# Two squared-relu sections merged, small loads a stage ahead, and contractions padded to 128 rows

## The chip, the cores and the metric

The kernel runs on one core of one Trainium2 chip. The metric is the device time of one launch in microseconds, 2791.74 before the change. Five engines work side by side, each through its own instructions in order: TensorE (PE: matrix products and transposes), VectorE (DVE), ScalarE (ACT), GpSimd (POOL) and SyncE (SP), which here only issues transfers between the chip's main memory and the on-chip memory (SBUF). TensorE writes its results to banks of a small accumulator memory (PSUM), and VectorE or ScalarE takes them from there.

## What is computed

A sequence of 512 tokens of width 1024 goes through two blocks, all in float32. The first block has two layers, latent attention with a squared-relu part and then a gated recurrence with another. The second block adds three mixers (sparse attention with a top-k index, "dsa"; compressed, selected and windowed attention, "nsa"; a state-space scan, "ssd") and ends with a squared-relu part of its own.

```python
def sq_relu_mlp(h, w1, w2):            # 1024 -> 4096 -> 1024
    a = jax.nn.relu(h @ w1)
    return (a * a) @ w2

for layer in range(DEPTH):             # DEPTH = 2: mla_mixer, then hgrn2_mixer
    ...
    h = h + rms_norm(m, norm_gains[layer, 1])
    a = rms_norm(h, norm_gains[layer, 2])
    h = h + rms_norm(sq_relu_mlp(a, mlp_w1[layer], mlp_w2[layer]), norm_gains[layer, 3])

# second block
u = rms_norm_2(x, norm1_g) @ w_in      # split into the inputs of the mixers
# dsa: idx = relu(iq . ik) weighted by iw (8 heads of 32), top-k keys, softmax over them
# nsa: blocks = a[:, win_idx] + pos; compress = einsum('bnlgd,lde->bnge', blocks, w)
# ssd: dt = softplus(dt + dt_bias); a = -exp(a_log); a_cum = cumsum(dt * a)
#      y_diag from exp(a_cum_i - a_cum_j), then the scan over 4 chunks of 128 tokens
```

## The kernel before

**Stages.** `build` (L2040) runs five stages one after another: the latent attention, the first squared-relu part (`mlp0`, about 232 to 584 us in the trace), the recurrence (`hgrn`, to 892 us), the second squared-relu part (`mlp1`, to 1253 us) and the second block (`b2`). The tokens are in NT = 4 blocks of 128. The input of a stage lies transposed in SBUF as `xT`, in a high and a low part.

**Products.** A float32 product is three matmuls of rounded parts: high by high, high by low, low by high (`mm3`, L124 to L126). Weights arrive as `raw` tiles over the one queue of SP and are split by `chunk`: ScalarE casts the high part (L209), VectorE or GpSimd subtracts the low part (L210; GpSimd while the last token blocks of a stage are still to be moved). `raw` tiles come from a ring of two (`wr`), chunks from a ring of four (`wc`), or, for the first ones of a stage, from a pool of large tiles (`b8`).

**A squared-relu stage** (`mlp`, L511) runs eight sections. Section s computes 512 of the 4096 hidden columns with `dense_a` (weights moving, the transposed input fixed), evacuates them by relu, square and split into `hT` (L524 to L527), and multiplies them by 512 rows of `w2` with `run_section`. The result has two halves of 512 columns per token block, each a sum over 4 k-tiles of 128, added to the accumulator `acc` by VectorE (L440; the first section copies by ScalarE, L438).

**The bridge** (`bridge`, L428) joins a stage to the next. After each half of a token block in the last section it squares and sums (`half`, L462), takes the reciprocal root on ScalarE and VectorE (L160 to L163), multiplies by a gain (L478, GpSimd for the first two token blocks), updates the residual h (L487) and writes the next stage's normalized input (L494). One token block later `move` (L502) transposes it on TensorE (L399) and splits it again (L129, L130). The moves of the last two blocks are left to the next stage's first products.

**The second block** begins with `dense_b` for the columns that dsa needs (`first[tb]`). `ssd_consts` (L1602) is called there: it loads the small operands of the scan (`conv_w`, `conv_b`, `norm_g` through a transpose, L176 to L180; `dsk` by two loads L1613, 64 partitions by 16 single elements each; `dtb` and `na` as rows repeated over 128 partitions, L1116) and `time_steps` (L1633) computes dt and its sums on VectorE, ScalarE and TensorE. `dsa` (L1262) and `nsa` (L1369) load small gains of their own (`gk`, `gqd`, `pos`). In dsa the index queries and keys are packed as high, low, high in `ipk` (three parts of 32 columns: 96 rows after the transposes L1294 and L1300) for the index products L1314. In nsa a compressed value `vc4` of 32 rows stands four times, and L1586 multiplies 32 of its 128 rows; the compressed keys and values come from `mm3` over split sums `bs` (L1480, L1481). TensorE has matmuls of later weights ("fill") between these steps.

What sets the order: a scheduler places the instructions on each engine when the kernel is built, so the tables of the section on the change show the built order.

## Time and profile before

| | us |
|---|---|
| runs shown | 2789.57, 2791.74, 2791.75; median 2791.74 |
| profiled execution | 2790.97, its span 2789.3, granted TensorE clock 0.983 of full |
| busy in the span | TensorE 2656.4 (95%), VectorE 1641.2 (59%), ScalarE 1211.7 (43%), GpSimd 496.4 (18%) |
| chain of work that ended last | TensorE 80%, VectorE 11%, ScalarE 4%, issue 2%, transfers 1%, GpSimd 1% |

The chain is followed back from the last instruction, each step to what released it. TensorE is on it four fifths of the time; what the other engines hold of it are the places where TensorE stands idle and waits for them, and these are found in the list of waits and in the timelines of single engines. The granted clock of a stretch tells whether TensorE's matmuls ran at its upper level there.

### The profile page before, as it was taken

To read this page: it belongs to the slowest core of one execution; us is meant where nothing else is said; L and a number is where in the kernel's file an instruction comes from. 1 tells how busy PE (TensorE), PEld (TensorE's weight loads), DVE (VectorE), ACT (ScalarE), POOL (GpSimd) and SP (SyncE) were. 2 spreads that over 40 slices of the span, in tenths; PEclk is the share of its full clock that TensorE was granted. 3 is DMA by queue.
4 is the path that set the end of the run, shared out by engine and by line. 5 is a ranking of instruction groups with operands and counts; after the bars stand their busy time and mean duration, and the time that the engine had idled before them with its cause. 6 is when DMAs were issued, how large, how long until landed. Compare 5 with 4: busy or idle time off the path is not lost.

```text
span 2789.3 us, 35203 instructions
## 1 busy us (share of the span) xinstructions
PE 2656.4 (95%) x13393; PEld 2190.2 (79%) x13393; DVE 1641.2 (59%) x3231; ACT 1211.7 (43%) x2389; POOL 496.4 (18%) x370
## 2 busy tenths in 40 slices
PE   7999999989999999996899989989999999999999
PEld 6888888868888888875677777777788887888887
DVE  6755444466565444453976659759748774544444
ACT  5555222245454322232457536636645652232222
POOL 1010000020002000012322213212365556200000
PEclk9999999999999999998999999999999999999999
DMA  4232322322233223323331231211152335222332
GB/s 138 61 121 76 101 96 91 106 69 83 69 114 106 91 91 101 96 88 97 99 92 47 89 88 57 61 57 50 59 183 84 108 112 181 98 91 91 104 93 76
DMA packets 281965, 259.09 MB, mean 93 GB/s; under 512 B 39436, under 2 KB 224068, under 8 KB 281796
## 3 DMA queue, kind: packets, MB, share of 16 engines
q1 hardware_dynamic: 281796, 256.84, 29.7%
q8 instruction: 105, 1.72, 0.3%
q14 instruction: 64, 0.52, 0.1%
HBM read 234.79 MB, written 22.02 MB: 92 GB/s over the span
## 4 chain that ended last, share of the span: by engine, by line
PE 80%; DVE 11%; ACT 4%; issue 2%; DMA 1%; POOL 1%; SPq 0%; ACTq 0%; DVEq 0%; POOLq 0%
PE pm L124 20%; PE pm L125 20%; PE pm L126 20%; PE po L606 2%; PE psc L126 2%; PE psc L124 2%; PE psc L125 2%; PE pt L601 2%; PE psc L1896 1%; PE psc L1060 1%; ACT wch L209 1%; DMA gk<-in_dsa_k_norm_dram 1%; PE pt L399 1%; POOL wch L210 1%; DVE qraw L1161 1%
## 5 line engine op out<-in xcount | busy, mean ns | idle before, releaser
L209 ACT CAST wch<-raw 128x1024 fp32r<-128x1024 f32 (+3 forms) x393 | 407.6, 1041 | 497.3 <-PE pm L126 392.6
L124 PE MATMUL pm<-xT,wch 128*128 128x512 f32 (+1 forms) x1568 | 597.9, 383 | 2.2 <-ACT xT L129 1.5
L125 PE MATMUL pm<-xT,wch 128*128 128x512 f32 (+1 forms) x1568 | 596.3, 381 | 0.9 <-DVE xT L130 0.9
L126 PE MATMUL pm<-xT,wch 128*128 128x512 f32 (+1 forms) x1568 | 595.4, 380 | 1.3 <-POOL wch L210 1.3
L210 DVE TENSOR_TENSOR wch<-raw,wch 128x1024 fp32r<-128x1024 f32 (+1 forms) x266 | 325.5, 1225 | 196.7 <-ACT wch L209 196.3
L210 POOL TENSOR_TENSOR wch<-raw,wch 128x1024 fp32r<-128x1024 f32 (+3 forms) x127 | 307.9, 2429 | 702.2 <-ACT wch L209 669.7
L124 PEld LDWEIGHTS pm<-xT,wch 128*128 128x128 f32 x1568 | 296.4, 190 | 55.2 <-ACT xT L129 3.2
L126 PEld LDWEIGHTS pm<-xT,wch 128*128 128x128 f32 x1568 | 297.4, 190 | 53.4 <-POOL wch L210 1.7
L125 PEld LDWEIGHTS pm<-xT,wch 128*128 128x128 f32 x1568 | 297.7, 190 | 52.4 <-DVE xT L130 2.0
L124 PE MATMUL pm<-wch,hT 128*128 128x512 f32 x768 | 300.1, 393 | 0.2 <-ACT hT L526 0.2
L125 PE MATMUL pm<-wch,hT 128*128 128x512 f32 x768 | 295.5, 390 | 0.0
L126 PE MATMUL pm<-wch,hT 128*128 128x512 f32 x768 | 295.5, 390 | 0.0
L525 DVE SCALAR_TENSOR_TENSOR f<-pm,r 128x512 f32<-128x512 f32 x96 | 66.4, 691 | 249.8 <-ACT r L524 249.6
L524 ACT ACTIVATE r<-pm 128x512 f32<-128x512 f32 x96 | 57.4, 598 | 322.4 <-PE pm L126 322.4
L124 PEld LDWEIGHTS pm<-wch,hT 128*128 128x128 f32 x768 | 144.2, 188 | 38.0 <-ACT hT L526 8.8
L126 PEld LDWEIGHTS pm<-wch,hT 128*128 128x128 f32 x768 | 143.5, 188 | 31.0
L125 PEld LDWEIGHTS pm<-wch,hT 128*128 128x128 f32 x768 | 144.2, 188 | 29.2
L478 POOL TENSOR_TENSOR acc<-acc,g 128x512 f32<-128x512 f32 x16 | 21.3, 1335 | 695.9 <-ACT bj L462 353.4
L562 ACT ACTIVATE p<-p,mn 128x128 f32<-128x128 f32 x224 | 125.7, 566 | 20.9 <-DVE mn L560 19.8
L440 DVE TENSOR_TENSOR acc<-pm,acc 128x512 f32<-128x512 f32 x112 | 77.1, 689 | 95.5 <-PE pm L126 95.1
L130 DVE TENSOR_TENSOR pT<-pt,pT 128x512 fp32r<-128x512 f32 x224 | 100.5, 485 | 30.1 <-ACT pT L129 28.1
L129 ACT CAST pT<-pt 128x512 fp32r<-128x512 f32 x224 | 86.0, 428 | 45.1 <-PE pt L601 29.6
(570 smaller groups left out, 4857.2 us busy)
## 6 DMA issues: line engine op xcount, KB each, us to landing
raw<-in_mlp_w_dram SPq DMA_DIRECT2D x64, 1024.0 KB, 5.3
raw<-in_w_in_dram SPq DMA_DIRECT2D x64, 512.0 KB, 3.7
raw<-in_w_ff_dram SPq DMA_DIRECT2D x32, 1024.0 KB, 5.2
raw<-in_hgrn_w_in_dram SPq DMA_DIRECT2D x24, 512.0 KB, 4.2
raw<-in_w_in_dram SPq DMA_DIRECT2D x8, 1024.0 KB, 5.9
raw<-in_w_br_ssd_dram SPq DMA_DIRECT2D x16, 512.0 KB, 4.2
gd<-fo SPq DMA_DIRECT2D x24, 256.0 KB, 2.3
fg<-gd SPq DMA_DIRECT2D x24, 256.0 KB, 3.1
```

What stands on the lines that cost most here:

```text
L124: mm(p, ah, bh, start=start, stop=False)
L125: mm(p, ah, bl, start=False, stop=False)
L126: mm(p, al, bh, start=False, stop=stop)
L129: self.nc.scalar.copy(h, src)
L130: self.nc.vector.tensor_sub(l, src, h)
L209: self.nc.scalar.copy(w[:, 0], raw)
L210: (self.nc.gpsimd if self.late and LP else self.lo).tensor_sub(w[:, 1], raw, w[:, 0])
L440: self.nc.vector.tensor_add(d, p, d)
L524: nc.scalar.activation(r, p, AF.Relu)
L525: nc.vector.scalar_tensor_tensor(f, p, 0.0, r, op0=ALU.max, op1=ALU.mult)
L562: nc.scalar.activation(p, p, AF.Exp, bias=mn[:, b:b + 1], scale=-1.0, accum_out=sm[:, b:b + 1])
L601: nc.tensor.transpose(t[:, (b - kb) * 128:(b - kb + 1) * 128], p[b][:, kb * 128:kb * 128 + 128], self.ident)
```

## The change

Sections 6 and 7 of `mlp0` and `mlp1` become one: section 6 keeps its `hT`, and after section 7's `dense_a` one `run_section` sums over 8 k-tiles of 128. Its second column half takes its chunks from a pool of four (`mlpw`) in `mlp0`, and from the pool of large tiles in `mlp1`. `ssd_consts` becomes `small_operands`; it is called at the start of `mlp1`, and the gains and positions of dsa and nsa are loaded there as well. The adds of `dtb` stay at the start of the second block; the rest of `time_steps` becomes part of `late_sums`, which is called behind the top-k. `ipk` gets four parts, so the index products contract 128 rows; `vc4` holds its 32 rows in four places of a zeroed 128-row tile; `acumT` and `sel` go from 96 rows to 128. The compressed keys and values are 16 plain float32 matmuls instead of 48 of split parts.

```diff
     def chunk(self, raw, pool=None, early=False):
-        if early:
+        if early or pool is self.big:
...
-    def mlp(self, X, w1, w2, g_out, g_next, alloc=None):
+    def mlp(self, X, w1, w2, g_out, g_next, alloc=None, begin=None):
...
+            if begin:
+                begin(self.sc, tmp)
+            X2 = lambda tiles: lambda k, hl: tiles[k // 4][hl][:, k % 4]
+            held = []
...
+                held.append(hT)
+                if s == 6 and g_out is not None:
+                    continue
+                pools = None, None
                 if s == 7:
                     if g_out is not None:
                         bridge = self.bridge(st, acc, g_out, g_next, alloc)
+                        pools = None, self.big if alloc else self.pool("mlpw", 4, st)
...
-                self.run_section(w2, s * 4, lambda k, hl: hT[hl][:, k], 4,
-                             self.add_to(acc, s == 0 and g_out is not None), (lambda: bridge) if bridge else None)
+                n = len(held)
+                self.run_section(w2, (s + 1 - n) * 4, X2(held), 4 * n,
+                                 self.add_to(acc, s == 0 and g_out is not None), (lambda: bridge) if bridge else None, pools)
+                held = []
...
-                self.ssd_consts(sc, first)
+                self.time_steps(first)
...
-                    pk = ip.tile([128, 9, 3, 32], F32R, name="ipk")
+                    pk = ip.tile([128, 9, 4, 32], F32R, name="ipk")
...
+                    for a in range(2):
+                        nc.scalar.copy(pq[:, :, a, 0], src[:, 0:8])
+                    nc.vector.tensor_sub(pq[:, :, 0, 1], src[:, 0:8], pq[:, :, 0, 0])
+                    nc.vector.tensor_sub(pq[:, :, 1, 1], src[:, 0:8], pq[:, :, 0, 0])
...
-                self.late_sums()
                 self.normed_keys(ip, kraw, 1, NT, lambda i: gk, lambda i: kh[:, 0], lambda i: kl[:, 0])
...
                     nc.vector.tensor_scalar(ix, ix, -2e38, -NEG, op0=ALU.is_gt, op1=ALU.mult)
+                self.late_sums()
...
-                    w = self.chunk(self.raw(A["nsa_cmp_w_2"][0, i].rearrange("(k l) d e -> (l d) k e", l=2)))
+                    w = self.raw(A["nsa_cmp_w_2"][0, i].rearrange("(k l) d e -> (l d) k e", l=2))
...
-                    bs = ip.tile([128, 2, 16, 32], F32R, name="bs")
-                    nc.scalar.copy(bs[:, 0], bl)
-                    nc.vector.tensor_sub(bs[:, 1], bl, bs[:, 0])
                     p = self.sbank()
                     for k in range(16):
-                        self.mm3(p[:32, :64], bs[:, 0, k], bs[:, 1, k], w[:, 0, k], w[:, 1, k], k == 0, k == 15)
+                        nc.tensor.matmul(p[:32, :64], bl[:, k], w[:, k], start=k == 0, stop=k == 15)
...
+                        nc.gpsimd.memset(vc4.bitcast(F32), 0.0)
                         for a in range(4):
-                            nc.scalar.copy(vc4[32 * a:32 * a + 32], vc)
+                            nc.scalar.copy(vc4[32 * a:32 * a + 32, a], vc)
...
-                    r = slice(32 * (i % 4), 32 * (i % 4) + 32)
                     for hl in range(2):
-                        nc.tensor.matmul(po, vc4[r], pcT[i // 4][r, hl], start=hl == 0, stop=False)
+                        nc.tensor.matmul(po, vc4[:, i % 4], pcT[i // 4][:, hl], start=hl == 0, stop=False)
...
-    def ssd_consts(self, pl, first):
+    def small_operands(self, pl, tmp):
...
+        dk = self.bc_row(pl, A["dsa_k_norm_2"][0], 64, "gk")
+        dq = raw("r")
+        nc.sync.dma_start(dq[:, :64], bc_rows(A["dsa_q_norm_2"][0], 64))
+        nc.sync.dma_start(dq[:, 64:], bc_rows(A["nsa_q_norm_2"][0], 64))
...
-            at = pl.tile([96, S], F32R, name="acumT")
-            sel = pl.tile([96, 32], F32R, name="sel")
+            at = pl.tile([128, S], F32R, name="acumT")
+            sel = pl.tile([128, 32], F32R, name="sel")
...
-            rb = self.fl.tile([128, S], F32, name="rb", tag="rb", bufs=1)
+            rb = self.b8([4, S], F32, "rb")[:, 0]
...
+            k.sc = k.pool("sc", 1, right, side="right")
...
-                X = k.mlp(X, A["mlp_w1"][j], A["mlp_w2"][j], ng[j, 3], g, alloc(nxt))
+                X = k.mlp(X, A["mlp_w1"][j], A["mlp_w2"][j], ng[j, 3], g, alloc(nxt), k.small_operands if nxt == "b2" else None)
```

ScalarE at the end of the first squared-relu stage, before: squares and sums of the bridge (L462, of `acc` and of h), reciprocal roots (L160), casts of moved blocks (L129) and of the next stage's weights (L209).

```order
L462 ACTIVATE bj,bss<-acc 128x512
L209 CAST wch<-raw 128x1024
L462 ACTIVATE bj,bss<-h 128x512
L160 ACTIVATE ry<-bs_4832,eps 128x1
L462 ACTIVATE bj,bss<-h 128x512
L129 CAST xT<-pt 128x4x128
L209 CAST wch<-raw 128x1024
L160 ACTIVATE ry<-bs_4848,eps 128x1
L129 CAST xT<-pt 128x4x128
L462 ACTIVATE bj,bss<-acc 128x512
```

The same place in the changed kernel.

```order
L462 ACTIVATE bj,bss<-h 128x512
L160 ACTIVATE ry<-bs_4795,eps 128x1
L462 ACTIVATE bj,bss<-h 128x512
L209 CAST wch<-raw 128x1024
L160 ACTIVATE ry<-bs_4811,eps 128x1
L209 CAST wch<-raw 128x1024 x3
L462 ACTIVATE bj,bss<-acc 128x512
L129 CAST xT<-pt 128x4x128
L462 ACTIVATE bj,bss<-acc 128x512
L129 CAST xT<-pt 128x4x128
```

The four casts of weights stood among three steps of the chain before, and stand around one reciprocal root now; on TensorE the second of the four moves stands 15 matmuls behind the first before and 48 now.

SP at the start of the second squared-relu stage, before: the gains of the bridge, the weights of the stage, the gains of the next bridge.

```order
L452 DMA g_7129<-in_norm_gains_dram 128x1024
L455 DMA g_7131<-in_norm_gains_dram 128x1024
L200 DMA raw<-in_mlp_w_dram 128x8x256 x2
L200 DMA raw<-in_mlp_w_dram 128x4x512 x2
L452 DMA g_9623<-in_norm_gains_dram 128x1024
L455 DMA g_9625<-in_norm_g_dram 128x1024
```

The same place in the changed kernel, from the bridge's second gain on.

```order
L455 DMA g_7119<-in_norm_gains_dram 128x1024
L1612 DMA dsk<-in_ssd_d_dram 64x16x1 x2
L1128 DMA dtb<-in_ssd_dt_bias_dram 128x32
L1128 DMA na<-in_ssd_a_log_dram 128x32
L1128 DMA gk<-in_dsa_k_norm_dram 128x64
L1633 DMA gk_7484<-in_nsa_k_norm_dram 128x64 x3
L200 DMA raw<-in_mlp_w_dram 128x8x256 x2
L200 DMA raw<-in_mlp_w_dram 128x4x512 x2
L176 DMA r<-in_ssd_conv_w_dram 96x128
L176 DMA r<-in_ssd_conv_b_dram 24x128
```

The small loads stand between the bridge's gains and the stage's first weights, and behind these come the inputs of the scan's convolution.

ScalarE at the same place, before: the split of the last weights of the recurrence, its accumulator copies and squares.

```order
L209 CAST wch<-raw 128x1024 x4
L438 COPY acc<-pm 128x512
L209 CAST wch<-raw 128x1024
L462 ACTIVATE bj,bss<-acc 128x512
L438 COPY acc<-pm 128x512
L209 CAST wch<-raw 128x1024 x2
L438 COPY acc<-pm 128x512
L462 ACTIVATE bj,bss<-acc 128x512 x2
L160 ACT_TABLE_LOAD
```

The same place in the changed kernel, where L1617 is the exponential of `na`.

```order
L209 CAST wch<-raw 128x1024 x4
L1617 ACTIVATE na<-na 128x32
L438 COPY acc<-pm 128x512
L462 ACTIVATE bj,bss<-acc 128x512
L438 COPY acc<-pm 128x512
L209 CAST wch<-raw 128x1024 x2
L438 COPY acc<-pm 128x512
L462 ACTIVATE bj,bss<-acc 128x512
L209 CAST wch<-raw 128x1024
L160 ACT_TABLE_LOAD
```

The exponential stands ahead of the first copy L438, and one cast L209 comes later by two rows.

## Rows read from the trace of the kernel before

**Rows 1.** The page, part 1: busy us (share of span) and instructions.
```profile
PE 2656.4 (95%) x13393; PEld 2190.2 (79%) x13393; DVE 1641.2 (59%) x3231; ACT 1211.7 (43%) x2389; POOL 496.4 (18%) x370
```

**Rows 2.** Timeline of TensorE: start, us, what, [idle before, releaser], three places.
```profile
594.07 1.94 PE L399 MATMUL pt<-ident,acc 128*128 128x128 f32 x8 [9.95 <-DVE acc L494]
...
1261.86 1.94 PE L399 MATMUL pt<-ident,acc 128*128 128x128 f32 x8 [9.04 <-DVE acc L494]
...
1330.64 0.34 PE L1294 MATMUL pt<-identr,ipk 128*96 128x128 f32 x1 [24.62 <-DVE ipk L1291]
```

**Rows 3.** Busy time by windows: us, then each engine, PEclk, DMA share, GB/s.
```profile
584.00:598.00 14.00, 4.05 (x15) 3.48 (x15) 13.21 (x16) 5.77 (x12) 8.99 (x8) 0.64 0.36 113
1305.00:1336.00 31.00, 6.38 (x28) 5.14 (x27) 15.14 (x46) 8.95 (x25) 8.16 (x4) 0.56 0.39 122
1700.00:1790.00 90.00, 89.23 (x519) 72.72 (x518) 79.42 (x262) 68.83 (x198) 25.39 (x22) 1.00 0.10 27
```

**Rows 4.** Timeline of VectorE and of GpSimd at the end of the first squared-relu stage.
```profile
591.10 3.48 DVE L494 SCALAR_TENSOR_TENSOR acc<-h,ry,g 128x512 f32<-128x512 f32 x2
...
588.22 5.16 POOL L210 TENSOR_TENSOR wch<-raw,wch 128x1024 fp32r<-128x1024 f32 x2 [2.50 <-issue]
```

**Rows 5.** Timeline of VectorE at the start of the second block.
```profile
1318.81 0.39 DVE L1639 TENSOR_TENSOR fo<-psc,dtb 128x32 f32<-128x32 f32 x3 [21.86 <-DMA gk<-in_dsa_k_norm_dram]
```

**Rows 6.** DMA issues, 1284 to 1324 us: count, KB each, median us to landing.
```profile
dsk<-in_ssd_d_dram SPq DMA_DIRECT2D x2, 4.0 KB, 18.6
...
na<-in_ssd_a_log_dram SPq DMA_DIRECT2D x1, 16.0 KB, 19.9
```

**Rows 7.** Timeline of SyncE's DMA issues at both places.
```profile
843.56 0.34 SPq L455 DMA_DIRECT2D g<-in_norm_gains_dram  x1
...
1293.63 1.44 SPq L1613 DMA_DIRECT2D dsk<-in_ssd_d_dram  x2
...
1299.01 1.15 SPq L1116 DMA_DIRECT2D na<-in_ssd_a_log_dram  x1
```

**Rows 8.** Timeline of ScalarE at the end of the recurrent stage.
```profile
865.57 0.59 ACT L438 COPY acc<-pm 128x512 f32<-128x512 f32 x1 [5.11 <-PE pm L126]
```

**Rows 9.** TensorE's waits, 855 to 912 us: us in total, times, longest.
```profile
PE pt L399 <- DVE acc L494: 2.9, 2, 1.7
```

**Rows 10.** The page, parts 5 (busy, mean ns, idle) and 6 (us to landing).
```profile
L209 ACT CAST wch<-raw 128x1024 fp32r<-128x1024 f32 (+3 forms) x393 | 407.6, 1041 | 497.3 <-PE pm L126 392.6
...
L210 DVE TENSOR_TENSOR wch<-raw,wch 128x1024 fp32r<-128x1024 f32 (+1 forms) x266 | 325.5, 1225 | 196.7 <-ACT wch L209 196.3
...
raw<-in_mlp_w_dram SPq DMA_DIRECT2D x64, 1024.0 KB, 5.3
```

**Rows 11.** Timeline of TensorE around matmuls over 32 rows.
```profile
1687.02 0.40 PE L125 MATMUL pm<-xT,wch 128*128 128x512 f32 x1
1687.35 0.49 PE L1586 MATMUL po<-pcT,vc 32*128 32x512 f32 x1
1687.77 0.50 PE L126 MATMUL pm<-xT,wch 128*128 128x512 f32 x1
1688.10 0.40 PE L124 MATMUL pm<-xT,wch 128*128 128x512 f32 x1
1688.34 0.39 PE L125 MATMUL pm<-xT,wch 128*128 128x512 f32 x1
...
1721.45 0.73 PE L1586 MATMUL po<-pcT,vc 32*128 32x512 f32 x2
1722.11 0.92 PE L606 MATMUL po<-pT,vsw 128*128 128x512 f32 x3
```

**Rows 12.** Groups by line and form, L1586: count, ns least, median, most.
```profile
L1586 PE MATMUL po<-pcT,vc x32: 382/492/590, 1686.0 to 1986.6; 32*128 32x512 f32 x32
```

**Rows 13.** TensorE's waits over the whole span.
```profile
PE psc L124 <- ACT bs L1480: 3.5, 2, 2.1
...
PE psc L126 <- DVE bs L1481: 1.7, 1, 1.7
```

More of the change, by code (lines that the diff above doesn't have):

```diff
@@ L1623, in ssd_consts, with time_steps @@
                                 channel_multiplier=-1)
-        ones = pl.tile([128, 128], F32, name="ones2")
+        ones = pl.tile([128, 1], F32, name="ones2")
         nc.gpsimd.memset(ones, 1.0)
-        cwf = cw.rearrange("p a b -> p (a b)")
-        nc.vector.tensor_scalar(cwf, cwf, 0.5, None, op0=ALU.mult)
-        self.sc = cw, gn, dsk, tri, ones, *self.time_steps(pl, tri, ones, dtb, na, first)
-    def time_steps(self, pl, tri, ones, dtb, na, first):
+        dk = self.bc_row(pl, A["dsa_k_norm_2"][0], 64, "gk")
+        dq = raw("r")
+        nc.sync.dma_start(dq[:, :64], bc_rows(A["dsa_q_norm_2"][0], 64))
+        nc.sync.dma_start(dq[:, 64:], bc_rows(A["nsa_q_norm_2"][0], 64))
+        nc.vector.scalar_tensor_tensor(dk, dk, -0.125, dq[:, :64], op0=ALU.mult, op1=ALU.mult)
+        gk = pl.tile([128, 3, 64], F32, name="gk3")
+        for i in range(3):
+            nc.sync.dma_start(gk[:, i], bc_rows(A["nsa_k_norm_2"][0, i], 64))
+        nc.vector.tensor_mul(gk, gk, dq[:, None, 64:].to_broadcast([128, 3, 64]))
+        nc.vector.tensor_scalar(gk, gk, -0.125, None, op0=ALU.mult)
+        posr = tmp.tile([128, S], F32, name="f")[:16, :256].rearrange("p (a c) -> p a c", a=2)
+        pos = pl.tile([128, 2, 16], F32, name="pos")
+        for i in range(2):
+            nc.sync.dma_start(posr[:, i], A["nsa_cmp_pos_2"][0, i].rearrange("(k l) d -> k (l d)", l=2))
+        t = self.tbank()
+        for i in range(2):
+            nc.tensor.transpose(t[:, i * 16:i * 16 + 16], posr[:, i], self.ident[:16, :16])
+        nc.vector.tensor_copy(pos, t[:, :32].rearrange("p (i k) -> p i k", k=16))
+        steps = tuple(pl.tile([128, NT, 32], F32, name=n) for n in ("dt", "acum", "dtd", "cd"))
+        self.sops = (cw, gn, dsk, tri, ones, *steps), dtb, na, dk, gk, pos
+    def time_steps(self, first):
         nc = self.nc
-        dt, acum, dtd, cd = (pl.tile([128, NT, 32], F32, name=n) for n in ("dt", "acum", "dtd", "cd"))
+        (_, _, _, tri, ones, dt, acum, dtd, cd), dtb, na = self.sops[:3]
         q, x = (self.fl.tile([128, S], F32, name=n, tag=n) for n in ("fg", "fo"))
@@ L1676, in ssd @@
             xt8 = lambda shape, dt, name: xp.tile([128] + shape, dt, name=name, tag="b8")
-            cw, gn, dsk, tri, ones, dt, acum, dtd, cd = self.sc
+            cw, gn, dsk, tri, ones, dt, acum, dtd, cd = self.sops[0]
             def conv(m, p, c):
@@ L1697, in conv @@
                 return c
[L1700 to L1702 removed]
+            at = pl.tile([128, S], F32R, name="acumT")
+            sel = pl.tile([128, 32], F32R, name="sel")
+            for a in range(4):
                 nc.scalar.copy(sel[32 * a:32 * a + 32], self.ident[:32, :32])
@@ L1911, in ssd_pair @@
             t = self.tbank()
-            nc.tensor.matmul(t, sel[:, h:h + 1].to_broadcast([96, 128]), at, start=True, stop=True)
+            nc.tensor.matmul(t, sel[:, h:h + 1].to_broadcast([128, 128]), at, start=True, stop=True)
             L = tr("L")
```

86 lines of the change are left out of this document (35 added, 51 removed).

## The prediction

> **What bounds the kernel now.** I read the totals first [rows 1]: TensorE works 2656.4 of 2789.3 us, so a local edit can win only idle TensorE time, slow-clock time or matmul time. The profiled execution took 2790.97 us, 1.7 more than its span; the median of the runs shown is 2791.74, 0.8 more, so a sum made against the profiled one stands for both within 0.1%. Next I read the three longest idle stretches of TensorE [rows 2]: 9.95 us at the end of the first squared-relu stage, 9.04 at the end of the second, and 24.62 in the first microseconds of the second block. Together they are 43.6 of 132.9 idle us. Work at the half clock follows them [rows 3]: the mean granted clock over the first and the third stretch is 0.64 and 0.56 (its levels are 1.2 and 2.4 GHz), where in the attention of the second block 89.23 of 90 us are busy at 1.00.
>
> What ends last in each? At the ends of the stages it is VectorE's L494, the next stage's normalized input [rows 4]. Two L494 take 3.48 us, while GpSimd runs the weight-splitting subtractions of L210, two of them in 5.16. So the idle 9.95 us is a chain of short VectorE steps that GpSimd stretches, with too few products left to cover it. At the start of the second block it is a transfer: VectorE's first add on dtb waited 21.86 us [rows 5]. The two dsk loads, of 4 KB each at most, land 18.6 us after issue, and the loads queued behind them (na 19.9 us) wait too [rows 6, 7].
>
> **Part A, sections 6 and 7 in one.** It removes eight accumulator adds per stage, beside TensorE's work: worth nothing. What counts is the bridge. A token block's products were 24 matmuls by 0.23 us [rows 11] = 5.5 us; with 8 k-tiles they are 48, 11 us, so the chain for one block hides under the next block's products, and 48 instead of 15 matmuls lie between the first two moves. Yet the four casts of the next stage's weights and their L210 still stand ahead of block 1's L162, L163 and L494, so the stretched steps remain. The nearest row is the end of the recurrent stage, whose last products already have 8 k-tiles: 2.9 us in two waits [rows 9]. I take 3.4 left of each gap.
>
> Per stage, the old loss is the gap and about 2 us of work at half clock after it (4.05 us busy in the first stretch [rows 3], most of it at half speed): 12 and 11. The new section has a wait of its own. Four raw weight tiles are wanted where two were, and the ring holds two. The third is asked for when the second has been split, so the path is split 1.04 + 1.22, landing 5.3, split 2.26 [rows 10]: 9.8 us, against 36 matmuls by 0.23 = 8.2 us. That leaves 1.6, taken as 2 in the first stage. In the second stage the chunks come from the pool that still holds the input of dense_a, and two casts wait ahead of the last relu; by the same rows 1.04 us for the relu and about 3.5 for a chunk's cast, subtraction and first use, 4.6 together. Clock dips, up to 2 us for each wait that remains or is new, as after the old gaps, take 2.5 and 2. Gain 12 - 3.4 - 2 - 2.5 = 4.1 and 11 - 3.4 - 4.6 - 2 = 1: **5 us**. Bounds: 20 when only the recurrent stage's 2.9 us remains of 23; 5 lost when the chain keeps its length and the new waits come on top.
>
> **Part B, small operands a stage ahead.** Start of the second block: the 24.62 us gap loses its cause. What is next? TensorE has 21 fill matmuls, 4.8 us, before the first index transpose. In the new order VectorE's adds need no transfer and the index subtraction comes twelve rows behind them, some 3 us. I expect 0 to 2 us left, and 2 us more come back from the half clock (6.38 us busy in 31 at 0.56 [rows 3]): gain **25**, bounds 18 and 29.
>
> Start of the second squared-relu stage pays. The loads now stand on SP behind g1 and g2, the second issued at 843.56 [rows 7], and ahead of the four weight loads. dsk would be asked for at about 844.4. From dsk's issue, 1293.63, to na's landing, 1299.01 + 19.9, it took 25.3 us [rows 6, 7], some 2 of them behind two weight tiles, so na lands at 867 to 870. On ScalarE na's Exp now stands ahead of the first accumulator copy L438, which ran at 865.57 after 5.11 idle us [rows 8] and freed the bank that TensorE's next product needs. So TensorE stops for 2 to 4.5 us; the evacuations, L462 and casts queued behind the Exp come as much later, and so do the weight loads, which now wait for dsk's landing near 863 (844.4 + 18.6). With one dip and the first square and sum of the bridge coming late: **7 lost**, bounds 0 (na lands by 865.5) and 14 (the 4.5 us are paid a second and a third time at the two moves, with a dip). The transposes of conv_w and pos stand inside the stage's first dense part, whose loads land near 900 us; 0 to 3, I take **1 lost**. na's other use, the time steps, moves behind the top-k with cover by fill matmuls: nothing.
>
> **Part C, 128-row contractions.** Thirty-two matmuls L1586 contract 32 rows [rows 12]. From the matmul before an isolated one the starts are 0.33, 0.42 and 0.33 us apart, and then 0.24 between 128-row neighbours [rows 11]: 1.08 - 3 x 0.23 = 0.39 lost. A pair takes 0.66 where 0.46 would do (last two lines of [rows 11]); with 0.10 on either side as above that is 0.40. Four single and fourteen paired places make 18 by 0.40 = 7.2. TensorE has no slack there (89.23 of 90 us busy [rows 3]), VectorE has some (79.42): of 7.2 I take **6**, bounds 3 and 7.2. The 96-row contractions are left at nothing.
>
> The row speaks against overlap: two 32-row matmuls in a row take 0.66 us, not the time of one. The Trainium skill ("TensorE: Matmul & The Clock Gate", Why this matters for your kernels) advises the opposite of this change, slicing small contractions into separate 32-row groups because such matmuls then run concurrently. Here both of a pair sit in one group, so no overlap was there to lose; had it been, the pairs' overlap would be lost, 14 by 0.23 = 3.2 us slower instead of 6 faster, and the sum would be 2768. The Trainium skill ("TensorEngine Tiling (Array Packing)", Key Properties) states that changing the tiling mode drains TensorE, which this trace's 0.33 and 0.42 us at a change, against 0.24, agree with.
>
> The compressed keys lose the cast L1480 and subtraction L1481, and GpSimd's chunk subtraction; TensorE waited 3.5 and 1.7 us for these two [rows 13]. What is next is the 16 adds on VectorE ahead of them, so part stays: **4**, bounds 2 and 7 with the dips. Their matmuls fall from 48 cheap ones to 16 in plain float32, whose price here I bound at plus or minus 1. More copies for the 128-row index tiles lie beside fill matmuls: nothing.
>
> Sum: 2790.97 - 5 - 25 + 7 + 1 - 6 - 4 = **2759**; by the parts' bounds, not all at one end, 2745 to 2775.
>
> **Rivals.** First, the merge hides nearly everything and na comes in time: A 20, B 26, C 10, 2735. For it: the recurrent stage's small waits. Against it: the two-tile ring.
>
> Second, the wait for dsk moves rather than goes: SP, ScalarE and the weight tiles stall at the second squared-relu stage for 20 us instead of 8. Then 2790.97 - 5 - 25 + 20 + 1 - 10 = 2772. For it: the dsk loads are as small and as scattered there. Against it: ScalarE is free from 860 to 865 us, so most of the landing is covered.
>
> Third, the merge does not do what it says: the chain keeps both gaps whole and the new waits of 2 + 4.6 with a dip each are added: 10 lost in place of 5 gained, 2774.
>
> Fourth, slower than before: na's Exp at the head of ScalarE's order. The other terms gain 39; so it decides from a landing later than about 905 us, 39 us behind the copy at 865.57. If the DMA engines served the two first weight loads along with dsk (10.6 us) and dsk itself took twice its 18.6, na would land near 899: 33 us, with the 14 of the moves 47, and 2799. Against it: dsk is first in the queue.
>
> **How the numbers follow.** Forecast 0.54, first rival 0.16, second 0.13, third 0.12, fourth 0.03; 0.02 for anything else. The likeliest gives 2759. The range reaches down to 2742, most of the way to the first rival, and up to 2778, past the second and third. About 0.2%, 5.6 us, is what a measurement of this kernel can tell from no change: faster holds the forecast, the first and most of the two middle rivals, 0.91; same 0.05, from the middle rivals together; slower 0.04.
>
> **What would show it.** A: waits for L494 at the ends near 3 us, and a wait on a chunk in the merged section's second half. B: no idle stretch above 3 us at the index transposes, dsk's landing some 18 us after an issue near 844, and a TensorE wait near 866. C: starts 0.23 us apart around the matmuls that were L1586 (L1582 in the changed kernel). The forecast is wrong if the gaps at the stages' ends are still 9 us, if the stall near 866 exceeds 10, or if the attention of the second block does not shorten by some 3 us per group.

## The result, and the profile after

The changed kernel takes 2746.7 us, the median of four runs (2743.34 to 2748.76), against 2791.74: ratio 0.9834 [0.9816, 0.9853], 45 us faster. The forecast was 2759 in a range of 2742 to 2778: the direction was right and the range held the time, but the forecast was 12 us too slow. The profiled execution took 2748.3 us, 1.7 more than its span. Both profiled executions stand within 2 us of their medians, so differences between the two traces can be read as differences of the kernels. Executions of one kernel lie up to 16 us apart, the longer ones at a lower granted clock (a_only, below: 2771 to 2773 us at 0.987 or 0.988, 2782 to 2785 at 0.982), so a difference of medians is good to some 5 us, and the leads in the traces are read beside it.

From the page of the changed kernel, its span and its part 1, which answers to [rows 1]:

```profile
span 2746.6 us, 35061 instructions
...
PE 2652.5 (97%) x13329; PEld 2192.9 (80%) x13329; DVE 1619.0 (59%) x3211; ACT 1204.4 (44%) x2382; POOL 498.6 (18%) x373
```

TensorE's busy time fell by only 3.9 us (64 matmuls fewer) and the span by 42.7. Nearly all of the gain is idle TensorE time: 132.9 us before, 94.1 now.

The list of TensorE's waits in the changed kernel (engine, what waits, releaser: us in total, times, longest), of three windows: the ends of the first and the second squared-relu stage, and the start of the second block. They answer to the three rows of [rows 2], of 9.95, 9.04 and 24.62 us.

```profile
PE pt L399 <- DVE acc L494: 3.1, 2, 2.1
```
```profile
PE pt L399 <- DVE acc L494: 2.1, 2, 1.9
```
```profile
PE pt L1307 <- DVE ry L153: 5.3, 1, 5.3
PE pt L1307 <- DVE rt L151: 1.3, 1, 1.3
```

Each of the three shrank and none went to nothing. At the end of the recurrent stage, where [rows 9] had 2.9 us of waits, the same list (855 to 912 us) now has a new first line:

```profile
PE pm L124 <- ACT acc L438: 4.3, 1, 4.3
```

For a balance, take the moment at which the same piece of TensorE's work starts in both traces; their difference is the changed kernel's lead.

| place | before, us | after, us | lead | change of lead |
|---|---|---|---|---|
| end of the latent attention, last move | 239.9 | 239.5 | 0.4 | |
| end of first squared-relu stage, last move | 619.3 | 610.9 | 8.4 | +8.0 |
| end of recurrence, last move | 910.9 | 910.4 | 0.5 | -7.9 |
| end of second squared-relu stage, last move | 1282.5 | 1274.0 | 8.5 | +8.0 |
| second block, first index product | 1336.4 | 1298.3 | 38.1 | +29.6 |
| dsa, last product with its values | 1564.6 | 1535.1 | 29.5 | -8.6 |
| nsa, keys | 1595.9 | 1563.4 | 32.5 | +3.0 |
| nsa, first product with vc4 | 1686.0 | 1646.1 | 39.9 | +7.4 |
| nsa, last one of the first group | 1776.0 | 1731.3 | 44.7 | +4.8 |
| nsa, last one of the second group | 1986.6 | 1937.5 | 49.1 | +4.4 |
| end | 2785.2 | 2742.8 | 42.4 | -6.7 |

Part of the lead at the start of the second block is order, not gain. Busy time by windows over that stretch (us; then PE, PEld, DVE, ACT, POOL busy with counts; PE clock, DMA share, GB/s), the kernel before and then the changed one:

```profile
1282.50:1336.40 53.90, 27.34 (x120) 21.73 (x119) 17.74 (x52) 15.24 (x33) 15.69 (x7) 0.75 0.43 122
```
```profile
1274.00:1298.30 24.30, 16.20 (x74) 12.52 (x71) 19.15 (x49) 12.07 (x28) 11.96 (x5) 0.89 0.85 249
```

TensorE's idle time goes from 26.6 to 8.1 us, 18.5 less. Busy time falls by 11.1, because 46 matmuls of fill no longer stand ahead of the first index product; they are still done, later. At 0.227 us each these are 10.4 us, which leaves 0.7 for the better clock. The next stretch, to the last product of dsa, shows where they went:

```profile
1336.40:1564.60 228.20, 216.25 (x1119) 172.19 (x1117) 172.21 (x460) 137.44 (x327) 63.28 (x68) 0.99 0.24 69
```
```profile
1298.30:1535.10 236.80, 224.32 (x1163) 178.74 (x1162) 173.09 (x461) 140.06 (x330) 66.60 (x69) 0.99 0.24 69
```

The changed kernel does 44 matmuls more there, at about the same idle time (12.0 and 12.5 us), and the lead falls from 38.1 to 29.5 us. So the start of the second block is worth 29.5 - 8.5 = 21 us, of which 18 are idle time. The 6.7 us given back at the end are of the same kind: behind the second attention group of nsa, TensorE does 27 matmuls more than before, which the groups no longer hold.

### The profile page after: what moved, and what is told of

Same layout as the page of the kernel before. It is cut to its first block, busy times and chain, and to the rows that moved or that the text cites. A ratio compares the mean times of both kernels' runs of the same rounds, so it can differ in the third digit from the quotient of the medians.

```text
span 2746.6 us, 35061 instructions
## 1 busy us (share of the span) xinstructions
PE 2652.5 (97%) x13329; PEld 2192.9 (80%) x13329; DVE 1619.0 (59%) x3211; ACT 1204.4 (44%) x2382; POOL 498.6 (18%) x373
## 5 line engine op out<-in xcount | busy, mean ns | idle before, releaser
L124 PE MATMUL pm<-xT,wch 128*128 128x512 f32 (+1 forms) x1568 | 598.1, 383 | 3.1 <-ACT xT L129 1.5
L209 ACT CAST wch<-raw 128x1024 fp32r<-128x1024 f32 (+3 forms) x389 | 402.6, 1041 | 448.1 <-PE pm L126 349.8
L210 POOL TENSOR_TENSOR wch<-raw,wch 128x1024 fp32r<-128x1024 f32 (+3 forms) x127 | 308.2, 2433 | 673.1 <-ACT wch L209 624.0
L210 DVE TENSOR_TENSOR wch<-raw,wch 128x1024 fp32r<-128x1024 f32 (+1 forms) x262 | 320.2, 1225 | 184.7 <-ACT wch L209 183.8
L124 PEld LDWEIGHTS pm<-xT,wch 128*128 128x128 f32 x1568 | 296.3, 190 | 55.8 <-ACT xT L129 3.2
L124 PE MATMUL pm<-wch,hT 128*128 128x512 f32 x768 | 300.1, 393 | 0.0
L124 PEld LDWEIGHTS pm<-wch,hT 128*128 128x128 f32 x768 | 144.3, 188 | 36.4 <-ACT hT L530 7.1
L574 ACT ACTIVATE p<-p,mn 128x128 f32<-128x128 f32 x224 | 125.5, 564 | 20.5 <-DVE mn L572 19.5
L440 DVE TENSOR_TENSOR acc<-pm,acc 128x512 f32<-128x512 f32 x96 | 66.1, 689 | 99.5 <-PE pm L126 99.2
L129 ACT CAST pT<-pt 128x512 fp32r<-128x512 f32 x224 | 85.3, 427 | 44.8 <-PE pt L613 30.0
```

The lines of the kernel that those rows point to most:

```text
L124: mm(p, ah, bh, start=start, stop=False)
L129: self.nc.scalar.copy(h, src)
L209: self.nc.scalar.copy(w[:, 0], raw)
L210: (self.nc.gpsimd if self.late and LP else self.lo).tensor_sub(w[:, 1], raw, w[:, 0])
L440: self.nc.vector.tensor_add(d, p, d)
L574: nc.scalar.activation(p, p, AF.Exp, bias=mn[:, b:b + 1], scale=-1.0, accum_out=sm[:, b:b + 1])
```

## Experiments

The theory after the result: the merge made the gain at the two ends by covering a chain that GpSimd stretches; the small operands made the gain at the second block and the new wait near 862 us; the compressed keys made most of the rest. Rivals: the gain at the ends came with the moved loads; dsk was late by its place in the queue and not by its 2048 elements; the chain was too long without any stretching; the attention groups were shortened by the 128-row vc4. Medians are of 4 to 7 runs, ratios against runs of the kernel before on the same chip.

**a_only**: the kernel before with the merge alone. It tells whether the merge or the moved loads made the gain at the ends.

```diff
+                if s == 6 and g_out is not None:
+                    continue
...
-                self.run_section(w2, s * 4, lambda k, hl: hT[hl][:, k], 4,
-                             self.add_to(acc, s == 0 and g_out is not None), (lambda: bridge) if bridge else None)
+                self.run_section(w2, (s + 1 - n) * 4, X2(held), 4 * n,
+                                 self.add_to(acc, s == 0 and g_out is not None), (lambda: bridge) if bridge else None, pools)
```

> The kernel before with the merged sections 6 and 7 alone. By my prediction the merge gives 5 us (4.1 and 1): 2787. By the trace of the changed kernel the last moves of the two stages came 7.9 and 8.1 us earlier, so the theory now is that nothing new waits in the merged section and only the end gaps of some 3 us are left: 16 less, 2776. Rival: the 24.6 us wait at the start of the second block is set by transfers, so what the second stage wins is waited away there: 8 less, 2784.

Measured: 2777.88, ratio 0.9949 [0.993, 0.9968], 14 us faster (9 to 20). TensorE's waits at the end of the first stage, and the first index transpose in its timeline (start, us, what, [idle before, releaser]):

```profile
PE pt L399 <- DVE acc L494: 3.1, 2, 2.1
```
```profile
1313.37 0.34 PE L1306 MATMUL pt<-identr,ipk 128*96 128x128 f32 x1 [24.36 <-DVE ipk L1303]
```

The merge alone cuts the end's wait to the 3.1 us of the changed kernel and leaves the wait of the second block whole. The index transpose starts 17.3 us ahead of [rows 2], 7.3 of them from the end of the first stage and 8.2 from that of the second, and the lead is 17 us at the end as well: the gain at the second stage is not waited away, and that rival falls. This is the profiled execution (2773.49); by the interval the median's 14 us are good to some 5.

**b_only**: the changed kernel without the merge, with the old 32-row vc4 and the old split matmuls of the compressed keys; the small operands and the index products stay changed.

```diff
-                held.append(hT)
-                if s == 6 and g_out is not None:
-                    continue
...
-            vc4 = pl.tile([128, 4, 128], F32R, name="vc4")
+            vc4 = pl.tile([128, 128], F32R, name="vc4")
...
-                        nc.tensor.matmul(p[:32, :64], bl[:, k], w[:, k], start=k == 0, stop=k == 15)
+                        self.mm3(p[:32, :64], bs[:, 0, k], bs[:, 1, k], w[:, 0, k], w[:, 1, k], k == 0, k == 15)
```

> The changed kernel with the sections separate and the two contractions of the compressed and selected attention as before: what is left is the small operands a stage ahead (and the 128-row index tiles and sums). By my prediction 25 - 7 - 1 = 17 less: 2775. By the trace of the changed kernel some 20 less at the second block's start and 8 more at the second squared-relu stage: 12 less, 2780. Rival, that the wait only moves: within 5 of 2792.

Measured: 2783.69, ratio 0.9965 [0.9952, 0.9977], 10 us faster (6 to 13). Its waits at the end of the first squared-relu stage, of the recurrence, and of the second squared-relu stage with the start of the second block:

```profile
PE pt L399 <- DVE acc L494: 10.0, 1, 10.0
```
```profile
PE pm L124 <- ACT acc L438: 4.3, 1, 4.3
```
```profile
PE pt L399 <- DVE acc L494: 9.0, 1, 9.0
PE pt L1297 <- DVE ry L153: 5.3, 1, 5.3
```

The two long waits at the ends are back, so they belong to the merge; the new 4.3 us and the left 5.3 stand unchanged, so they belong to the small operands. About 19 gained in one place and about 8 lost in the other leave 11, near the 10 measured.

**vc4_32**: the changed kernel with vc4 over 32 rows again.

```diff
-            vc4 = pl.tile([128, 4, 128], F32R, name="vc4")
+            vc4 = pl.tile([128, 128], F32R, name="vc4")
...
-                        nc.tensor.matmul(po, vc4[:, i % 4], pcT[i // 4][:, hl], start=hl == 0, stop=False)
+                        nc.tensor.matmul(po, vc4[r], pcT[i // 4][r, hl], start=hl == 0, stop=False)
```

> The changed kernel with vc4 and its matmuls over 32 rows again. If a change between 32 and 128 rows costs 0.40 us at 18 places and TensorE is the bound there, 6 to 7 us more than the changed kernel's 2747: 2753, with starts 0.33, 0.34 and 0.34 us apart around them again. Rival: VectorE bounds these stretches and what TensorE saves it waits: within 1 of 2747.

Measured: 2751.82, ratio 0.9856 [0.9841, 0.9872] against 0.9834 [0.9816, 0.9853]: 5 us slower than the changed kernel, with intervals that overlap. One place in TensorE's timeline, the changed kernel and then this one:

```profile
1677.43 0.40 PE L124 MATMUL pm<-xT,wch 128*128 128x512 f32 x1
1677.68 0.73 PE L1582 MATMUL po<-pcT,vc 128*128 128x512 f32 x2
1678.25 0.84 PE L618 MATMUL po<-pT,vsw 128*128 128x512 f32 x3
1678.93 0.27 PE L613 MATMUL pt<-ident,p 128*128 128x128 f32 x1
```
```profile
1677.98 0.40 PE L124 MATMUL pm<-xT,wch 128*128 128x512 f32 x1
1678.31 0.72 PE L1582 MATMUL po<-pcT,vc 32*128 32x512 f32 x2
1678.96 0.92 PE L618 MATMUL po<-pT,vsw 128*128 128x512 f32 x3
1679.71 0.28 PE L613 MATMUL pt<-ident,p 128*128 128x128 f32 x1
```

From the start of L124 to that of L613, over the same six matmuls, it is 1.50 us with 128 rows and 1.73 with 32: 0.23 saved at this pair, not the 0.40 of the prediction. Added up over all 17 places (15 pairs and 2 single ones), from the matmul ahead of each to the second one behind it, the starts span 16.6 us with 128 rows and 21.9 with 32: 5.3 us saved, 0.31 at a place. The two attention groups as a whole, with as many matmuls in both runs, are only 1.2 and 0.5 us longer with 32 rows, in the profiled execution, which was the fastest of its four (2749.56): most of what is saved in place is lost again within the groups. So the groups bear out 1.7 us, the medians 5, and these runs can't separate the two.

**cmp3**: the changed kernel with the split matmuls of the compressed keys.

```diff
-                    w = self.raw(A["nsa_cmp_w_2"][0, i].rearrange("(k l) d e -> (l d) k e", l=2))
+                    w = self.chunk(self.raw(A["nsa_cmp_w_2"][0, i].rearrange("(k l) d e -> (l d) k e", l=2)))
...
-                        nc.tensor.matmul(p[:32, :64], bl[:, k], w[:, k], start=k == 0, stop=k == 15)
+                    bs = ip.tile([128, 2, 16, 32], F32R, name="bs")
+                    nc.scalar.copy(bs[:, 0], bl)
+                    nc.vector.tensor_sub(bs[:, 1], bl, bs[:, 0])
...
+                        self.mm3(p[:32, :64], bs[:, 0, k], bs[:, 1, k], w[:, 0, k], w[:, 1, k], k == 0, k == 15)
```

> The changed kernel with the compressed keys and values as 48 matmuls of split parts again (cast, subtraction and chunk back). My prediction gave this edit 4 us: 2751. By the leads in the trace of the changed kernel around the two places (7.4 and 2.5 us of all edits there) up to 7: 2754. Rival: the wait for the sixteen adds ends last anyway, within 1 of 2747.

Measured: 2758.28, ratio 0.9877 [0.9861, 0.9892]: 11 us slower than the changed kernel, more than the 7 of the upper bound. TensorE's waits at the spot itself (of those from 1560 to 1960 us), the changed kernel and then this one:

```profile
PE psc L1480 <- DVE bl L1476: 2.6, 2, 1.4
```
```profile
PE psc L124 <- ACT bs L1479: 1.9, 1, 1.9
PE psc L126 <- DVE bs L1480: 1.7, 1, 1.7
```

They fall from 3.6 (the two lines of bs) to 2.6 (bl), a mere 1.0. Busy time by windows from the keys of the first group to its first product with vc4, in the same order:

```profile
1563.40:1646.10 82.70, 76.31 (x380) 60.89 (x380) 49.87 (x113) 29.32 (x49) 17.28 (x9) 0.90 0.44 122
```
```profile
1567.70:1656.50 88.80, 78.27 (x427) 62.83 (x427) 53.18 (x114) 30.78 (x52) 17.03 (x9) 0.90 0.35 89
```

TensorE's idle time in this stretch is 6.4 us in the changed kernel and 10.5 with the split matmuls; in the same stretch of the second group it is 6.8 and 9.7, and in the two attention groups together 3.6 and 6.2. Over the whole span it is 94.1 and 102.3, and TensorE's busy time is 3.2 us more. So most of the 11 us is idle time around the edit and not at it: in the list of waits those for qs (4.3 to 6.8), mn (1.6 to 4.1), pc (4.6 to 6.2) and kp (7.3 to 8.6) grow. How the removed steps reach these waits is not shown; the built order of the fill matmuls differs as well.

**dsk_before** and **dsk_after**: dsk as one row of 32 repeated over the partitions, then two VectorE copies, in place of two loads of single elements; in the kernel before and in the changed one.

```diff
-        d = A["ssd_d_2"][0]
+        dr = self.bc_row(pl, A["ssd_d_2"][0], 32, "dskr").rearrange("p (j e) -> p e j", e=2)
         for e in range(2):
-            nc.sync.dma_start(dsk[64 * e:64 * e + 64],
-                              bass.AP(tensor=d.tensor, offset=d.offset + e, ap=[[0, 64], [2, 16]]))
+            nc.vector.tensor_copy(dsk[64 * e:64 * e + 64], dr[64 * e:64 * e + 64, e])
```

> The kernel before, with dsk loaded as one row of 32 numbers repeated over the partitions and picked apart by two small VectorE copies, instead of 2048 single elements; nothing else is moved. If these single elements are what the loads behind them wait for, VectorE's adds come some 18 us sooner and the 24.6 us wait falls below 10: 2773 to 2780, as much as the whole part B. Rival, that the rows repeated over 128 partitions are slow by themselves: 2787 to 2792.

> The same edit on the changed kernel. If dsk is what makes na land at 861.6, na lands before the first accumulator copy at 857, the 4.3 us wait there and its half clock go, and 6 to 8 us fall: 2740. Rival, that the weight loads behind the other small loads set the start of the second squared-relu stage: 2745 to 2748.

Measured: dsk_before 2771.67, ratio 0.9923 [0.991, 0.9935], 21.5 us faster than before, twice what the whole of part B gives in b_only. Its DMA issues from 1284 to 1324 us (count, KB each, median us to landing) and TensorE's first wait from 1284 to 1330:

```profile
dskr<-in_ssd_d_dram SPq DMA_DIRECT2D x1, 16.0 KB, 3.4
dtb<-in_ssd_dt_bias_dram SPq DMA_DIRECT2D x1, 16.0 KB, 4.1
```
```profile
PE pt L1294 <- DVE ipk L1291: 4.2, 2, 3.6
```

The load of dtb, at the same place in the queue as ever, lands 4.1 us after its issue, and TensorE's wait of 24.6 is 4.2. So the small operands were never late because of their place: 2048 transfers of one element each in dsk kept the queue. The Trainium skill ("DMA: Bandwidth & Descriptors", Rules for kernel authors) states that a strided last dimension becomes one descriptor per element and is better rearranged; the 18.6 us of [rows 6] against 3.4 here agree, and so do the packets under 512 bytes in this window, 2834 before and 1090 here.

dsk_after, 2754.2, ratio 0.9853 [0.984, 0.9867], is no faster than the changed kernel. The 4.3 us wait near 862 is gone and the recurrent stage 7.6 us shorter, but the second block's plain matmuls run slower. Busy time of a steady stretch in the last squared-relu part, after_same (the changed kernel again, below) and dsk_after:

```profile
2420.00:2700.00 280.00, 280.00 (x1230) 229.92 (x1230) 128.85 (x153) 78.82 (x100) 0.00 (x0) 1.00 0.30 95
```
```profile
2420.00:2700.00 280.00, 280.00 (x1202) 225.12 (x1201) 125.93 (x151) 76.61 (x98) 0.00 (x0) 1.00 0.30 94
```

TensorE is busy throughout at full clock in both, and does 1230 matmuls in one and 1202 in the other: 0.2276 and 0.2329 us apart. TensorE's matmuls stand in the same order in both built kernels; what differs for them is the place of tiles in SBUF: the new tile dskr takes 128 bytes of each partition, and moves those behind it. pad128 tests that.

**lp0_before** and **lp0_after**: all subtractions L210 at the ends of stages go to VectorE, none to GpSimd.

```diff
-LP = 1
+LP = 0
```

> The kernel before, with the low parts of a next stage's first weights (L210) on VectorE at the ends of the stages instead of GpSimd. If GpSimd's subtractions stretch the short VectorE steps, the 9.95 and 9.04 us waits shrink by 3 to 5 us each: 2783. Rival, that these four subtractions of 1.2 us then stand in VectorE's own queue ahead of the chain: same within 3 of 2792, or slower.

> The same on the changed kernel, whose end waits are 2.1, 1.7 and 1.9 us. If these are still GpSimd's stretching, up to 1 us each and their half clock fall: 2742. Rival, that the covered chain has no room for 4.9 us more of VectorE work: 2747 to 2752.

Measured: 2769.6, ratio 0.9909 [0.9894, 0.9924], 25 us faster than before, more than twice what was expected; and 2734.38, ratio 0.9783 [0.977, 0.9796], some 12 us faster than the changed kernel. TensorE's waits at the ends of the first and the second squared-relu stage in lp0_before, where [rows 2] has 9.95 and 9.04:

```profile
PE pt L399 <- DVE acc L494: 3.0, 2, 2.6
```
```profile
PE pt L399 <- DVE acc L494: 2.3, 1, 2.3
```

In lp0_after no wait for L494 is left at either end. So the chain without stretching is still 2 to 3 us too long for the products of the kernel before, and not for the merged ones.

VectorE's timeline at the end of the first squared-relu stage, with GpSimd's beside it, in the changed kernel:

```profile
576.18 0.15 DVE L161 TENSOR_SCALAR rx<-bs 128x1 f32<-128x1 f32 x1
576.43 2.12 DVE L162 SCALAR_TENSOR_TENSOR rt<-ry,rx 128x1 f32<-128x1 f32 x1
578.58 2.32 DVE L163 SCALAR_TENSOR_TENSOR ry<-rt,ry 128x1 f32<-128x1 f32 x1
580.94 5.60 DVE L494 SCALAR_TENSOR_TENSOR acc<-h,ry,g 128x512 f32<-128x512 f32 x2
...
575.80 10.18 POOL L210 TENSOR_TENSOR wch<-raw,wch 128x1024 fp32r<-128x1024 f32 x4 [12.61 <-issue]
```

and in lp0_before, the same steps and one L210 on VectorE:

```profile
577.57 1.40 DVE L494 SCALAR_TENSOR_TENSOR acc<-h,ry,g 128x512 f32<-128x512 f32 x2
...
579.56 1.22 DVE L210 TENSOR_TENSOR wch<-raw,wch 128x1024 fp32r<-128x1024 f32 x1
...
581.36 0.21 DVE L162 SCALAR_TENSOR_TENSOR rt<-ry,rx 128x1 f32<-128x1 f32 x1
582.16 0.15 DVE L163 SCALAR_TENSOR_TENSOR ry<-rt,ry 128x1 f32<-128x1 f32 x1
```

While GpSimd subtracts, VectorE steps on one number per partition take 2.12 and 2.32 us in place of 0.21 and 0.15, and two L494 take 5.60 in place of 1.40; L161, which reads a single tensor, keeps its 0.15. At this end, four subtractions on VectorE cost 4 by 1.22 = 4.9 us; they save 4.2 on L494 and 4.1 on L162 and L163, and those stood on the chain. The Trainium skill ("SBUF — State Buffer", Who interferes with whom) states that a VectorE instruction with two SBUF inputs contends with a GpSimd instruction that reads SBUF, and that this contention is an exclusive lock; the stretched and the unstretched steps above agree. The wait that the merge covers with products can thus also be had by taking the stretching away. By the last moves in the traces, LP = 0 gains 10 and 6 us at the ends of the two squared-relu stages, where the merge gains 7 and 8; the 25 against the merge's 14 come from the other stages' ends, where LP = 0 acts too (1.6 us at the latent attention, 2.5 at the recurrence), and from medians that are good to some 5.

**pad128**: the changed kernel with an unused tile of 128 bytes in the pool of small operands.

```diff
+        pad = pl.tile([128, 32], F32, name="pad")
+        nc.gpsimd.memset(pad, 0.0)
```

> The changed kernel with one more, unused tile of 128 bytes per partition among the small operands, set to zero by GpSimd; it moves the tiles allocated behind it (the second block's input and the later weights) 128 bytes down, as the dsk row did, and changes nothing else. If the places of operands set the matmuls' rate, starts are 0.232 us apart from the second block on and the kernel takes 12 to 16 us more than the changed one: 2760. Rival, that the rate came from the dsk load or from that execution: 2747 and 0.227 us.

**after_same**: the changed kernel again, as the comparison on the same chip.

> The changed kernel itself, beside the other three on one chip: 2743 to 2749, ratio 0.983.

Measured: pad128 2760.18, ratio 0.9881 [0.9866, 0.9896]; after_same 2747.44, ratio 0.9836 [0.9823, 0.985]. The unused tile costs 12.7 us. The same window in pad128:

```profile
2420.00:2700.00 280.00, 280.00 (x1201) 224.90 (x1201) 126.37 (x153) 77.57 (x100) 0.00 (x0) 1.00 0.31 97
```

It is the pace of dsk_after (1202), not of the changed kernel (1230). In the built kernels the second block's transposed input starts at byte 191968 of a partition before the pad and at 191840 in pad128 and dsk_after, and the last weights' chunks move by the same 128 bytes; TensorE's order is the same matmul for matmul. In the window shown, of what the matmuls read only the chunks of weights (`wch`) lie elsewhere, and both kinds of matmul there read them, one moving and one fixed. So dsk_after lost by its tiles' places what it won at the load. Which rule of places makes the difference is open.

**dve_plus**: the changed kernel with five additions of 128 by 128 on VectorE for each of the 16 heads' steps of the attention in nsa.

```diff
+                    dz = pl.tile([128, 128], F32, name="dz", bufs=1)
+                    for _ in range(5):
+                        nc.vector.tensor_add(dz, sm[:, 0:128], sm[:, 128:256])
```

> The changed kernel with five more VectorE adds of 128 columns (some 0.28 us each) for each of the 16 heads of the compressed and selected attention, 22 us of VectorE work. If VectorE bounds those stretches (it is busy 94% there, and the 32-row matmuls' 0.4 us cost nothing), most of it shows: 2760 to 2768. Rival, TensorE is the bound: VectorE has 5 to 14 us of slack, 2750 to 2756.

Measured: 2772.34, ratio 0.9927 [0.9915, 0.994], 25 us slower than after_same. The additions in its list of groups (count, busy us, mean ns), and the first attention group, from the first to the last product with vc4, in after_same, in this run and in the kernel before, by windows:

```profile
L1582 DVE TENSOR_TENSOR dz<-slm 128x128 f32<-128x128 f32 x80 | 31.7, 397 | 0.1
```
```profile
1643.00:1728.30 85.30, 83.74 (x487) 68.25 (x487) 82.10 (x284) 68.00 (x202) 23.87 (x21) 1.00 0.11 29
```
```profile
1646.90:1748.20 101.30, 91.92 (x496) 71.49 (x496) 95.80 (x319) 69.14 (x200) 27.35 (x22) 0.98 0.12 32
```
```profile
1686.00:1776.00 90.00, 87.19 (x497) 69.83 (x496) 86.58 (x288) 70.34 (x205) 27.35 (x23) 1.00 0.14 41
```

31.7 us of work beside TensorE, more than the 22 expected, lengthen the two groups by 16 and 18.4 us, of which the kernel gets some back further on: it takes 25 more. So VectorE has no slack in the groups, being busy 82.10 of 85.30 us. In the kernel before it was as full: 86.58 of 90.00, the same 96%. The 79.42 of 90 in [rows 3] is of a window that begins 14 us into the group and ends 14 behind it. The reverse does not follow: TensorE is idle for only 1.6 us in this group and 2.1 in the second, so with this fill little is to be won there by less VectorE work. Nor does this run explain cmp3, whose idle time grows mostly ahead of the groups.

**best**: the changed kernel, LP = 0, and the dsk row in a scratch tile, which moves no other tile.

```diff
+        dr = raw("f")[:, :32]
+        nc.sync.dma_start(dr, bc_rows(A["ssd_d_2"][0], 32))
+        dr = dr.rearrange("p (j e) -> p e j", e=2)
...
-LP = 1
+LP = 0
```

> The changed kernel with L210 on VectorE at the ends of the stages and dsk loaded as one row into a scratch tile that is there anyway, so that no other tile's place in SBUF moves. The two gains were 12.4 us (2734) and 7.6 us at the second squared-relu stage: they lie at different places and add, 2727. If the slower matmuls of the second block in the run with dsk as a row of its own (starts 0.232 us apart instead of 0.227) come from the loads and not from the places of the tiles, they come back here: 2741.

Measured: 2726.9, ratio 0.9763 [0.975, 0.9776], 20.5 us faster than after_same. The copy of [rows 8] in ScalarE's timeline waits for its product alone again:

```profile
850.59 0.59 ACT L438 COPY acc<-pm 128x512 f32<-128x512 f32 x1 [4.98 <-PE pm L126]
```

LP = 0 alone gave 12; with the row in a place that moves nothing (the second block's input is at 191968 again), the load gives the 7 or 8 that dsk_after had hidden.

## Why the prediction was right, and where it was off

By the balance, A gave 11 us more than forecast, the second block 4 less and C 3 more. The errors offset in part, and what is left of them is the 10 to 12 us by which the forecast was too slow.

**A, 5 forecast, 14 to 16 measured** (a_only 14, the balance 8.0 in each stage). Right: the chain at the ends is shortened by cover, not removed, and 3.4 us were foreseen where 3.1 and 2.1 stand; the cause, GpSimd's stretching, is shown by lp0_before. The step that failed is "The new section has a wait of its own", 2 us in one stage and 4.6 in the other, each with a clock dip. ScalarE's timeline in the changed kernel shows the last chunks' cast:

```profile
544.10 2.00 ACT L209 CAST wch<-raw 128x1024 fp32r<-128x1024 f32 x2 [3.44 <-DMA raw<-in_mlp_w_dram]
```

ScalarE waits 3.44 us for the transfer, as the ring of two says it must, but the casts end at 546.1, the first subtraction at 546.4, and TensorE, which begins the section's products at 538.35, reaches these chunks 36 matmuls later, at about 546.5; no wait for a chunk stands in its list, in neither stage. The estimate began the 9.8 us path when the section begins; of its first term, a split of 2.26 us, all but 0.7 was done by then, so 8.1 us were left of it, against 8.2 of products. It just fits. With the 2 + 4.6 and their dips left out, the same sum gives 14 to 16, which is what was measured. The first rival, "the merge hides nearly everything" (20), was nearer on this term than the forecast; the third (10 lost) falls by a_only.

**B, second block: 25 forecast, 19 to 21 measured.** The wait lost its cause as said, but "I expect 0 to 2 us left" failed: 6.6 are left. VectorE's timeline there, with GpSimd's:

```profile
1286.81 0.16 DVE L152 TENSOR_TENSOR rt<-rt,rx 128x4 f32<-128x4 f32 x1
...
1288.43 2.15 DVE L152 TENSOR_TENSOR rt<-rt,rx 128x4 f32<-128x4 f32 x1
...
1291.38 1.64 DVE L153 SCALAR_TENSOR_TENSOR ry<-rt,ry 128x4 f32<-128x4 f32 x1
...
1288.17 7.25 POOL L210 TENSOR_TENSOR wch<-raw,wch 128x1024 fp32r<-128x1024 f32 x3 [4.23 <-ACT wch L209]
```

Steps on 128 by 4 numbers, 0.16 us a moment earlier, take 2.15 and 1.64 beside GpSimd's L210, and a third, L151 at 1293.15, takes 2.29. The prediction had the stretching in [rows 4] and did not ask whether the same pair meets here. LP = 0 does not reach these three L210, and the 5.3 us wait stands in lp0_after too, so this cause is read from one timeline and not tested. The result lies in the bounds, 18 to 29.

**B, second squared-relu stage: 7 + 1 lost forecast, 7.9 measured**, by the mechanism forecast. ScalarE's timeline and TensorE's at the place:

```profile
861.63 0.23 ACT L1617 ACTIVATE na<-na 128x32 f32<-128x32 f32 x1 [9.52 <-DMA na<-in_ssd_a_log_dram]
861.77 0.57 ACT L438 COPY acc<-pm 128x512 f32<-128x512 f32 x1
...
862.39 0.50 PE L124 MATMUL pm<-wch,oT 128*128 128x512 f32 x1 [4.29 <-ACT acc L438]
```

na's exponential waits 9.52 us for its load, the copy L438 stands behind it, and TensorE stops for 4.29, in the forecast's 2 to 4.5. Both the landing and the copy come some 8 us earlier than the forecast has them, which took its times from the trace before and left out the lead of the first merge; the wait is their difference and keeps its size. The second rival (20 lost) and the fourth (na after 905) fall: na lands at 861.6. That dsk is the cause, and not the place of the loads, is shown by dsk_after and dsk_before.

**C, 6 + 4 forecast.** The compressed keys gave 11, not 4. The step was right on its own wait (3.6 to 2.6 us) and wrong to end there: TensorE's idle time in the whole stretch from the keys to the groups falls by 4.1 and 2.9 us, and by 2.6 in the groups; why these other waits shrink too is open. For vc4 the term "18 by 0.40" = 7.2 came to 5.3 in place; the 6 kept of it are 1.7 by the groups and 5 by the medians. The words "VectorE has some" slack rest on a window that overlaps the group's end; over the group itself TensorE was busy 87.19 and VectorE 86.58 of 90.00 us, and it fits this that what vc4 saves in place shortens the groups only in part. The sign "shorten by some 3 us per group" came true in good part by luck: the groups went from 90.0 and 88.3 to 85.2 and 81.3 us, but they hold 11 and 14 matmuls fewer, which at 0.227 us each are 5.7 of these 11.8 us, and these are done elsewhere.

Sum by runs: 14 for A, 10 for the small operands of B, 11 and 2 to 5 for C make 37 to 40 of 45; the single parts' intervals, 4 to 5 us to either side, cover what is missing. Sum by the balance: 16 for A, 21 - 7.9 for B and 12.9 for all behind dsa, with 0.4 at the start, make its 42.4.

## What to carry to other kernels

Before a late load is moved, ask what it is made of: one row of dsk in place of 2048 single elements gave more where it was than the move did. A short VectorE step that takes ten times its usual while GpSimd works is not busy but shut out, and taking the cause away, one digit in the code, gave as much at the same two ends as covering it with products (16 us each), and more at the others. Before an engine is said to have slack in a stage, lay the window on the stage's own first and last instruction: a window 14 us off showed VectorE 79.42 of 90 us busy where the group's own showed 86.58. And when a stage gets shorter, count its matmuls: part of the gain may be work that has moved.

## What the runs showed of the chip

A tile's place changes the pace of matmuls. With 128 bytes more ahead of the second block's tiles, matmuls of 512 columns, in the same order, start 0.2331 us apart (280 us by 1201, pad128) instead of 0.2276 (by 1230, after_same), both at a granted clock of 1.00 and with TensorE busy all the time; 12.7 us over the whole kernel. Of what they read there, only the chunks of weights lie elsewhere. It hid a gain of 7 or 8 us in dsk_after, so a version that only adds a small tile is to be compared with one that adds it unused.
